# Seven units of yield behind the sample softmax, earlier high casts, and norm vectors on the load queue

## The chip, the cores and the metric

The kernel runs on one core of a Trainium2 chip. A core has TensorE (PE, matmuls and transposes), VectorE (DVE), ScalarE (ACT), GpSimd (POOL) and SyncE (SP); SP, ACT and POOL also issue DMA transfers, each from its own queue in program order. The metric is the device time in microseconds (us) of one execution, as a median of several.

## What is computed

One decoder layer for a prompt of 1024 tokens and a group of 8 x 4 sample tokens with a paged cache of 1024 tokens each. All in f32.

```python
aq, ak, av, bq, bk, bv, iq, ik, iw = split(rms_norm(x, g_mix) @ w_in)
# q, k of A and B: rms_norm per head of 64 (norm vectors q_norm_a, k_norm_a,
# q_norm_b, k_norm_b), then rotary positions; iq, ik: rotary positions
a_out = dsa_attention(aq, iq, iw, ik)   # softmax over the 256 best keys by
        # sum_h iw[h] * relu(iq[h] . ik), a top-k per query row
b_out = diff_attention(bq, bk, bv, lam) # softmax(q1 k1) - lam * softmax(q2 k2)
b_out = rms_norm(b_out, subln) * (1 - lam_init)
h = x + concat(a_out, b_out) @ w_out
y = h + hier_moe(rms_norm(h, g_ffn))    # 4 groups of 8 experts, 2 per token
```

The outputs are y and the new keys and values, of prompt and samples.

## The kernel before

A product in f32 is made of high and low parts: ACT casts a weight chunk to its high part (`wh`, L508), DVE (for one chunk of eight POOL) subtracts to get the low part (`wl`, L530), and PE runs high x high, high x low and low x high (L532, L533, L535 or L538).

**Projections, up to 465 us.** The columns of `w_in` come in sections of 512 columns: BV, the indexer's, BK, AV, BQ, AK, AQ. `section` (L500) casts its 8 chunks, then goes over the 8 prompt tiles of 128 tokens and evacuates each with `evac` (L372): ACT copies the PSUM result, norms and rotary positions follow on DVE and POOL (`m`, L340, and the norm vectors times the rotary table, `gtab`, L176, on POOL), and the last multiply with the reciprocal norm (L387) is POOL's in the two Q sections and DVE's in the K sections. The weights of a section are loaded on SP (`load_w`, called by `preload`) while the one before runs its next to last tile. `gains` loads a section's norm vector, three transfers on ACT's queue, held by `issue_after` until a copy. Beside the sections runs the selection of A's keys (scores, a bisection on POOL, DVE and ACT, and its end, L676 to L701); `mix` takes turns between such streams: it always advances the one whose sum of yields, divided by its total, is smallest. Behind AQ come the first transfers of attention: `open_pages` gathers pages of the cache on POOL's queue, and the queue of stores held back in `late` is emptied on SP (L1041).

**Attention, 465 to 931 us.** Two streams with a total of 280 each are mixed. `prompt_attention` runs B, then A, 8 query tiles each with 4 units per tile (scores L936 and L937 on PE, maxima on DVE, exp L940 on ACT, transposes L876, values L974 or L978), and writes each tile's result (`mo`, L1008, to `s_mix`, L1009 on SP). `samples` runs `sample_attention` for B and A: transposes of the queries and new keys (L1080, L1081) and their copies into `QB` (L1086) and `KN` (L1089), then for each of 2 groups the transposes of the pages (L1104), scores with `QB` (L1112) and with `KN` (L1120), the softmax (exp L1151 on ACT), its transposes (L876, `sc`), and values (`own`, L1165, L1169). Behind both it loads `w_out` through two buffers `raw` (L1219, 16 transfers on SP), casts the high parts (L1220, ACT) and subtracts the low parts (L1221, DVE).

**Output projection and router, 931 to 1079 us.** At its start ACT casts the samples' result `mixS` to its high part `msh` (L1282). The samples are projected first (L1325 to L1327).

**Experts, 1079 to 1402 us.** 24 groups; the weights stream in by DMA.

The order of the instructions on each engine is fixed before the program runs; it follows the order in which the streams are advanced.

Of the kernel before, what the change touches and what calls it, by code (L numbers as in the profile page):

```python
# [6 lines left out]
F32 = mybir.dt.float32  # L7
F32R = mybir.dt.float32r
# [4 lines left out]
ALU = mybir.AluOpType  # L13
# [109 lines left out]
def build(tc, a, upto=99, dbg=None):  # L123
# [185 lines left out]
    def gains(name, ap):  # L309

        g2 = tp.tile([P, 2, 64], F32, name="g2")
        with tc.issue_after(last_copy[0]):
            S.dma_start(g2[:, 0, :], bcast_row(ap[0], 64))
            S.dma_start(g2[:, 1, 0:32], bcast_row(ap[0, 32:64], 32))
            S.dma_start(g2[:, 1, 32:64], bcast_row(ap[0, 0:32], 32))
        gb[name] = g2

    def w2(name):
# [53 lines left out]
    def evac(sec, t, ps):  # L372
        r0, n = rows(t)
        att = sec[0]
        if sec[1] in "KQ":
            raw = w2("raw")
            S.copy(raw[:n], ps[:n])
            rr = tp.tile([P, 8], F32, name="rk")
            rms8(raw, n, rr[:n])
            tab = table(t, sec)  # L380
            ko = outs(t)
            rope(raw, n, 8, tab, ko, V)
            if sec[1] == "Q":

                V.tensor_scalar(rr[:n], rr[:n], 0.125 if t == NT else -0.125, None, op0=ALU.mult)
            E = G if sec[1] == "Q" and t < NT else V
            E.tensor_tensor(out=hd(ko[:n]), in0=hd(ko[:n]), in1=rr[:n].unsqueeze(2).to_broadcast([n, 8, 64]), op=ALU.mult)  # L387
            if sec[1] == "K":
                store(kd[att][r0:r0 + n], ko[:n])
            else:  # L390
                for u in range(2 if t < NT else 1):
                    store(qd[att][r0:r0 + n, :, u, :], hd(ko[:n]), 4)
        else:
            vn = outs(t)
            last_copy[0] = S.copy(vn[:n], ps[:n]).ins
            store(vd[att][r0:r0 + n], vn[:n])
# [70 lines left out]
    def score_tile(t):  # L467
# [29 lines left out]
        V.tensor_tensor(out=score[t][:, t * P:], in0=score[t][:, t * P:], in1=C("caus"), op=ALU.add)  # L497
        yield W * 0.0011

    def section(sec, ws, after=(), prep=False):  # L500

        WLG = (7,)
        evacuate = evac_iq if sec == "I" else lambda t, ps: evac(sec, t, ps)
        first = 2 if sec == "I" else 0
        wh, wl = [], []
        for kc in range(KC):
            wh.append(wp.tile([P, 512], F32R, name="wh", bufs=8))
            S.copy(wh[kc], ws[kc])  # L508
        for t in range(first, NT):
            if prep:  # L510
                if t + 2 < NT:
# [24 lines left out]
            if t == first:  # L536
                for kc in range(KC):
                    T_.matmul(ps, lhsT=xh[t][:, kc, :], rhs=wl[kc], start=False, stop=kc == KC - 1)  # L538
                s4 = w2("s4")
                S.copy(s4, smp)  # L540
                ps2 = acc()
                T_.matmul(ps2[:NS], lhsT=C("sum4"), rhs=s4, start=True, stop=True)
                evacuate(NT, ps2)
            evacuate(t, ps)
            if prep:
                evac_ik(t)
# [190 lines left out]


    SECS = ('BK', 'AV', 'BQ', 'AK', 'AQ')
    nxt = {}  # L740

    def preload(sec):
        def f():
            nxt[sec] = load_w(OFF[sec])
        return (f,)

# [40 lines left out]

    def sections():
        for i, sec in enumerate(SECS):
            if sec[1] != "V":  # L790
                gains(sec, a[f"{sec[1].lower()}_norm_{sec[0].lower()}"])
            yield from section(sec, nxt[sec], preload(SECS[i + 1]) if i + 1 < len(SECS) else (open_pages,))

    p2s = ExitStack()
# [88 lines left out]
    def prompt_attention(atts):  # L883
# [151 lines left out]
        V.tensor_tensor(out=le[:, 0:1], in0=le[:, 1:2], in1=le[:, 0:1], op=ALU.subtract)  # L1035
        V.tensor_scalar(neglam, le[:, 0:1], -0.2, None, op0=ALU.add)
        yield from advance(1, 1)

        while late:
            with tc.issue_after(holds[1]):  # L1040
                Y.dma_start(*late.pop(0))  # L1041
        behind = behind2 = None
        for i in range(len(tiles)):
            cur = nxt
            for u in range(4):
                ex = yield from scores(cur, u)
# [12 lines left out]
            if cur.t == NT - 1:  # L1059
                if behind2:  # L1060
                    yield from values(*behind2)
                behind2 = yield from turned(*behind)
                yield from values(*behind2)
                behind = behind2 = None
            yield from advance(i + 1, 99, True)
            before = cur
        yield from finish(before)

    def sample_attention(att):
# [5 lines left out]
            Y.dma_start(hd(qn[:NS]), qd[att][r0:r0 + NS, :, 0, :])  # L1075
            Y.dma_start(kn[:NS], kd[att][r0:r0 + NS])
        Y.dma_start(vn, vd[att][r0:r0 + NS])
        pt = tr()
        for c in range(4):
            T_.transpose(pt[:, c * NS:(c + 1) * NS], qn[:NS, c * P:(c + 1) * P], ident[:NS, :NS])  # L1080
            T_.transpose(pt[:, (4 + c) * NS:(5 + c) * NS], kn[:NS, c * P:(c + 1) * P], ident[:NS, :NS])  # L1081
        QB = sp_.tile([P, 4, 8, 8, 4], F32, name="QB", bufs=1)
        G.memset(QB, 0.0)
        for c in range(4):
            for s in range(2):
                V.tensor_copy(QB[64 * s:64 * s + 64, c, :, 2 * c + s, :],  # L1086
                              pt[64 * s:64 * s + 64, c * NS:(c + 1) * NS].rearrange("p (b q) -> p b q", q=4))
        KN = sp_.tile([P, 4, NS], F32, name="KN", bufs=1)
        V.tensor_copy(KN.rearrange("p c n -> p (c n)"), pt[:, 4 * NS:8 * NS])  # L1089
        kc_, vc_ = pages(att, "k"), pages(att, "v")  # L1090
        om = []
        for g in range(2):
            sc = sp_.tile([P, NTOK], F32, name="sc", bufs=1)

            for ch in range(4):
                raws = [early.pop(0) if early else page(kc_, ch, 4 * g + bb) for bb in range(4)]
                kts = []
                for r in range(2):
                    for bb in range(4):
# [5 lines left out]
                        evac_any(kt, pt.rearrange("p (c n) -> p c n", n=P))  # L1105
                        kts.append(kt)
                        yield 0.4
                sp = tr()
                for r in range(2):
                    for c in range(4):  # L1110
# [41 lines left out]
            S.activation(ex[:, 1024:], new, AF.Exp, bias=m2[:, 2:3], scale=1.0, accum_out=l2[:, 1:2])  # L1152
            V.tensor_tensor(out=l2[:, 2:3], in0=l2[:, 0:1], in1=l2[:, 1:2], op=ALU.add)
            V.reciprocal(l2[:, 3:4], l2[:, 2:3])
            pT = yield from transposed(ex, 8, "pT")
            ptn = tr()
            T_.transpose(ptn[:NS, :P], ex[:, 1024:], ident)
# [42 lines left out]
            V.tensor_copy(mixS[:, 4:8, :].rearrange("p c n -> p (c n)"), pt[:, :4 * NS])  # L1200

    p3w = ExitStack()
    woh, wol = [], []

    def samples():
        for att in "BA":
# [9 lines left out]
        for k in range(KC):  # L1216
            for q in range(2):
# [3 lines left out]
                V.tensor_tensor(out=wol[q][k], in0=w, in1=woh[q][k].bitcast(F32), op=ALU.subtract)  # L1221
                yield 1.5
        raw.close()

    mix((prompt_attention("BA"), 280), (samples(), 280))
    if "mix" in dbg:
# [50 lines left out]
    p3 = ExitStack()  # L1277
    fp = p3.enter_context(tc.tile_pool(name="fp", bufs=2, reuse_waits="tile"))
    sm = p3.enter_context(tc.tile_pool(name="sm", bufs=2, reuse_waits="tile"))
    msh = sm.tile([P, 8, NS], F32R, name="msh", bufs=1)  # L1280
    msl = sm.tile([P, 8, NS], F32R, name="msl", bufs=1)
    S.copy(msh, mixS)  # L1282
    V.tensor_tensor(out=msl, in0=mixS, in1=msh.bitcast(F32), op=ALU.subtract)
    ovi = cq.tile([P, NT + 1, 2], I32, name="ovi")
    ovv = cq.tile([P, NT + 1, 2, 3], I32, name="ovv")
    T2 = own()
# [18 lines left out]
    def project(t):  # L1305
# [7 lines left out]
            S.copy(mh, mx)  # L1313
            gtt(ml, mx, mh.bitcast(F32), ALU.subtract)
        else:
            mh, ml = msh, msl
        h = fp.tile([P, D], F32, name="xt")
        Y.dma_start(h[:n], xsrc(t))
        s1 = sm.tile([P, 4], F32, name="s1")
# [307 lines left out]
```

## Time and profile before

| | us |
|---|---|
| median of 3 timed runs | 1391.77 |
| lowest and highest of them | 1391.52, 1400.56 |
| the profiled execution | 1403.95 |
| its span, first to last instruction | 1402.1 |
| PE in use in the span | 1265.0 |
| DVE, ACT, POOL in use | 792.0, 561.5, 447.8 |

The profile's page has the busy time of each engine, and a chain of work that ended last; the share of PE in it is 44%. The trace behind the page can be asked for the same by stretches (windows), for an engine's waits and what ended them, and for an engine's instructions one by one (timeline). All times below are of the one profiled execution. A granted clock of 1.00 is PE's full level.

### The profile page before, as it was taken

To read this page: it belongs to the slowest core of one execution; us is meant where nothing else is said; L and a number is where in the kernel's file an instruction comes from. 1 tells how busy PE (TensorE), PEld (TensorE's weight loads), DVE (VectorE), ACT (ScalarE), POOL (GpSimd) and SP (SyncE) were. 2 spreads that over 40 slices of the span, in tenths; PEclk is the share of its full clock that TensorE was granted. 3 is DMA by queue.
4 is the path that set the end of the run, shared out by engine and by line. 5 is a ranking of instruction groups with operands and counts; after the bars stand their busy time and mean duration, and the time that the engine had idled before them with its cause. 6 is when DMAs were issued, how large, how long until landed. Compare 5 with 4: busy or idle time off the path is not lost.

```text
span 1402.1 us, 24778 instructions
## 1 busy us (share of the span) xinstructions
PE 1265.0 (90%) x9359; PEld 855.0 (61%) x9359; DVE 792.0 (56%) x2218; ACT 561.5 (40%) x1239; POOL 447.8 (32%) x505
## 2 busy tenths in 40 slices
PE   7999999997799689898889989999996999999994
PEld 4877675875467576776675776768884333333341
DVE  5544996969987677766655556946754111111110
ACT  5533666895432365544345555732220111111110
POOL 1012233254336534435236544321212112222101
PEclk9999999998899899999899999999997999999997
DMA  6223004133325765666467654347657999999992
GB/s 234 77 88 109 25 24 121 48 109 82 90 97 147 227 244 213 234 210 230 152 227 252 222 161 148 103 135 306 247 172 256 341 370 377 377 381 386 378 340 47
DMA packets 114149, 279.92 MB, mean 200 GB/s; under 512 B 50664, under 2 KB 50920, under 8 KB 101736
## 3 DMA queue, kind: packets, MB, share of 16 engines
q1 hardware_dynamic: 81248, 180.84, 35.4%
q0 software_dynamic: 26272, 95.43, 21.8%
q10 hardware_dynamic: 6504, 2.01, 0.6%
q8 instruction: 75, 1.23, 0.3%
q14 instruction: 50, 0.41, 0.1%
HBM read 234.33 MB, written 43.92 MB: 198 GB/s over the span
## 4 chain that ended last, share of the span: by engine, by line
PE 44%; DMA 9%; DVE 6%; issue 5%; POOL 3%; ACT 2%; SPq 0%; another core or an unknown queue 0%; POOLq 0%; ACTq 0%; DVEq 0%
PE acc L1513 9%; PE S L1533 4%; DMA wg<-in_w_exp_up_dram 4%; PE tr L1104 4%; PE tr L876 3%; PE acc L1325 3%; PE acc L1326 2%; PE acc L1327 2%; PE tr L1112 2%; PE own L1165 2%; PE acc L978 2%; DMA wg<-in_w_exp_gate_dram 2%; PE acc L974 2%; PE tr L936 2%; PE tr L937 2%
## 5 line engine op out<-in xcount | busy, mean ns | idle before, releaser
L532 PE MATMUL acc<-wh,xh 128*128 128x512 f32 x432 | 174.9, 405 | 15.3 <-ACT wh L508 15.3
L1513 PE MATMUL acc<-wg,xT 128*32 128x512 f32 x1536 | 174.7, 598 | 2.8 <-DMA wg<-in_w_exp_up_dram 2.4
L533 PE MATMUL acc<-wh,xl 128*128 128x512 f32 x432 | 172.1, 398 | 0.0
L940 ACT ACTIVATE mk<-mk,mx 128x256 f32<-128x256 f32 (+7 forms) x128 | 99.0, 775 | 83.4 <-DVE mx L938 74.0
L535 PE MATMUL acc<-wl,xh 128*128 128x512 f32 x320 | 126.6, 396 | 0.0
L1513 PEld LDWEIGHTS acc<-wg,xT 128*32 128x32 f32 x1536 | 54.6, 110 | 104.2 <-issue 95.5
L532 PEld LDWEIGHTS acc<-wh,xh 128*128 128x128 f32 x432 | 82.4, 191 | 48.0 <-ACT wh L508 25.8
L1528 DVE COPY aTe<-tr 128x256 f32<-128x256 f32 x24 | 10.2, 425 | 162.6 <-PE tr L1526 162.6
L533 PEld LDWEIGHTS acc<-wh,xl 128*128 128x128 f32 x432 | 82.5, 191 | 17.4 <-issue 1.2
L1533 PE MATMUL S<-wd,aTe 128*32 128x512 f32 x768 | 87.5, 594 | 4.3 <-DVE aTe L1528 3.3
L1508 DVE TENSOR_TENSOR xT<-tr,gc 128x512 f32<-128x512 f32 x48 | 32.9, 688 | 91.5 <-PE tr L1507 91.5
L1104 PE MATMUL tr<-cst,pg 128*128 128x128 f32 x512 | 78.8, 286 | 0.5 <-DVE ql L407 0.4
L936 PE MATMUL tr<-KS,qh 128*128 128x512 f32 (+3 forms) x192 | 75.1, 396 | 1.6 <-DVE aT L864 0.8
L1519 ACT ACTIVATE sg<-acc,its 128x256 f32<-128x256 f32 x24 | 11.4, 474 | 156.0 <-PE acc L1513 156.0
L1537 POOL DMA_INDIRECT out_o_y_dram<-yo,its x24 | 38.0, 1582 | 110.2 <-ACT yo L1536 66.1
L958 POOL TENSOR_SCALAR mk<-mk,rl 128x128 f32<-128x128 f32 (+7 forms) x64 | 49.3, 781 | 70.9 <-DVE rl L950 65.8
L1498 POOL DMA_INDIRECT xg<-s_hn,its x24 | 23.4, 977 | 142.4 <-PE tr L1507 128.9
L876 PE MATMUL tr<-cst,mk 128*128 128x128 f32 x432 | 65.1, 281 | 4.0 <-POOL mk L958 2.4
L535 PEld LDWEIGHTS acc<-wl,xh 128*128 128x128 f32 x320 | 60.9, 190 | 11.8
L937 PE MATMUL tr<-KS,ql 128*128 128x512 f32 (+3 forms) x192 | 66.2, 359 | 0.0
L1536 ACT ACTIVATE yo<-S,its 128x1024 f32<-128x1024 f32 x24 | 26.8, 1115 | 98.5 <-PE S L1533 98.5
L1104 PEld LDWEIGHTS tr<-cst,pg 128*128 128x128 f32 x512 | 61.6, 147 | 6.5 <-issue 2.0
(416 smaller groups left out, 2924.2 us busy)
## 6 DMA issues: line engine op xcount, KB each, us to landing
wg<-in_w_exp_gate_dram SPq DMA_DIRECT2D x32, 1024.0 KB
wg<-in_w_exp_up_dram SPq DMA_DIRECT2D x32, 1024.0 KB
wd<-in_w_exp_down_dram SPq DMA_DIRECT2D x32, 1024.0 KB
wr<-in_w_in_dram SPq DMA_DIRECT2D x56, 256.0 KB
xt<-in_x_prompt_dram SPq DMA_DIRECT2D x16, 512.0 KB
s_mix<-mo SPq DMA_DIRECT2D x16, 256.0 KB
qn<-s_qa SPq DMA_DIRECT2D x8, 512.0 KB
raw<-in_w_out_dram SPq DMA_DIRECT2D x16, 256.0 KB
```

The costliest lines, as they stand in the source:

```text
L532: T_.matmul(ps, lhsT=xh[t][:, kc, :], rhs=wh[kc], start=kc == 0 and t < NT - 1, stop=False)
L533: T_.matmul(ps, lhsT=xl[t][:, kc, :], rhs=wh[kc], start=False, stop=t == NT - 1 and kc == KC - 1)
L535: T_.matmul(ps, lhsT=xh[t][:, kc, :], rhs=wl[kc], start=False, stop=kc == KC - 1)
L876: T_.transpose(pt[:, (j - b) * P:(j - b + 1) * P], src[:, j * P:(j + 1) * P], ident)
L936: T_.matmul(sp[:, :c1 - c0], lhsT=T.qh[:, h * P:(h + 1) * P], rhs=KS[:, h, c0:c1], start=True, stop=False)
L937: T_.matmul(sp[:, :c1 - c0], lhsT=T.ql[:, h * P:(h + 1) * P], rhs=KS[:, h, c0:c1], start=False, stop=True)
L940: S.activation(mk[:, :W], mk[:, :W], AF.Exp, bias=mx[:, h:h + 1], scale=-1.0, accum_out=T.ll[:, h:h + 1])
L958: G.tensor_scalar(ex[s][:, :W], ex[s][:, :W], T.rl[:, 2 * u + s:2 * u + s + 1], 1.0, op0=ALU.mult, op1=ALU.mult)
L1104: T_.transpose(pt[:, c * P:(c + 1) * P], raws[bb][:, o_:o_ + P], ident)
L1325: T_.matmul(ps[:n], lhsT=mh[:, k, :], rhs=woh[q][k], start=k == 0, stop=False)
L1513: T_.matmul(gu[c:c + m, :].rearrange("p (u f) -> p u f", u=2), lhsT=xT[:, k, c:c + m], rhs=wg[:, :, k, :], start=k == 0, stop=k == KC - 1)
L1533: T_.matmul(py[c:c + m, q * 512:(q + 1) * 512], lhsT=aT[:, k, c:c + m], rhs=wd[:, k, q * 512:(q + 1) * 512], start=k == 0, stop=k == 1)
```

## The change

- `gains` issues on SP, without `issue_after`, and is called in `preload`, that is, one section earlier, ahead of the section's weights.
- In `evac` the last multiply of AQ's prompt tiles is DVE's; BQ's stays on POOL.
- `high` casts chunks of a section on demand: the first four of the next section are cast ahead of the evacuation of the last tile.
- The stores left in `late` are issued at the second prompt tile, in a plain loop.
- The queries' transposes and the `QB` and `KN` copies of the samples move behind the first eight page transposes.
- `yield 7` stands between the samples' exp and its transposes.
- The cast of `mixS` (now `ms`) moves from the start of the projection to the end of `samples`, behind the loads of `w_out`.

```diff
     def gains(name, ap):
         g2 = tp.tile([P, 2, 64], F32, name="g2")
-        with tc.issue_after(last_copy[0]):
-            S.dma_start(g2[:, 0, :], bcast_row(ap[0], 64))
...
+        Y.dma_start(g2[:, 0, :], bcast_row(ap[0], 64))
...
-            E = G if sec[1] == "Q" and t < NT else V
+            E = G if sec == "BQ" and t < NT else V
...
+    def high(ws, b, e):
+        got = whs.setdefault(id(ws), [])
+        for kc in range(b, e):
+            if len(got) == kc:
+                got.append(wp.tile([P, 512], F32R, name="wh", bufs=8))
+                S.copy(got[kc], ws[kc])
+        return got
...
-        wh, wl = [], []
-        for kc in range(KC):
-            wh.append(wp.tile([P, 512], F32R, name="wh", bufs=8))
-            S.copy(wh[kc], ws[kc])
+        wh, wl = high(ws, 0, KC), []
...
+            if t == NT - 1 and after and nxt_of(sec):
+                high(nxt[nxt_of(sec)], 0, 4)
             evacuate(t, ps)
...
     def preload(sec):
         def f():
+            if sec in SECS and sec[1] != "V":
+                gains(sec, a[f"{sec[1].lower()}_norm_{sec[0].lower()}"])
             nxt[sec] = load_w(OFF[sec])
...
-        while late:
-            with tc.issue_after(holds[1]):
-                Y.dma_start(*late.pop(0))
...
         for i in range(len(tiles)):
             cur = nxt
+            while i == 1 and late:
+                Y.dma_start(*late.pop(0))
...
+        def queries():
+            G.memset(QB, 0.0)
+            pt = tr()
...
+                if g == 0 and ch == 0:
+                    queries()
                 sp = tr()
...
             V.reciprocal(l2[:, 3:4], l2[:, 2:3])
+            yield 7
             pT = yield from transposed(ex, 8, "pT")
...
         raw.close()
+        mp = p3w.enter_context(tc.tile_pool(name="ms", bufs=1, side="right", reuse_waits="tile"))
+        msh, msl = [mp.tile([P, 8, NS], F32R, name=f"ms{u}") for u in range(2)]
+        S.copy(msh, mixS)
+        V.tensor_tensor(out=msl, in0=mixS, in1=msh.bitcast(F32), op=ALU.subtract)
+        ms.extend((msh, msl))
...
-    msh = sm.tile([P, 8, NS], F32R, name="msh", bufs=1)
...
-    S.copy(msh, mixS)
```

Three places in the order of the engines follow. Line numbers of the changed kernel are up to 23 higher (L876 of before is L890 there, L936 is L950).

PE, samples of A, first group, of before: from the last sample scores (`KN`, `QB`) to the first transposes of the exponentials (`sc`).

```order
L1120 MATMUL tr<-KN,QB 32x32 x16
L920 MATMUL tr<-idr,kst 128x128 x8
L1130 LDWEIGHTS repb
L1130 MATMUL tr<-selS,repb 128x512
L1130 LDWEIGHTS repb
L1130 MATMUL tr<-selS,repb 128x512
L1134 LDWEIGHTS repb
L1134 MATMUL tr<-selS,repb 128x32
L876 MATMUL tr<-cst,sc 128x128 x4
```

The same place of the change, the last eleven of the 33 rows that stand between: a prompt unit's scores (`KS`), values (`aT`, `VV`) and mask transposes (`mk`).

```order
L950 MATMUL tr<-KS,qh 128x384
L951 MATMUL tr<-KS,ql 128x384
L950 MATMUL tr<-KS,qh 128x384
L951 MATMUL tr<-KS,ql 128x384
L992 MATMUL acc<-aT,VV 64x128 x6
L890 MATMUL tr<-cst,mk 128x128 x6
L950 MATMUL tr<-KS,qh 128x512
L951 MATMUL tr<-KS,ql 128x512
L950 MATMUL tr<-KS,qh 128x512
L951 MATMUL tr<-KS,ql 128x512
L890 MATMUL tr<-cst,sc 128x128 x4
```

Where the sample scores were followed by seven rows of little work, several prompt units now stand ahead of `sc`.

POOL at the end of section AQ, of before: `m` and the multiplies (L387) of the last tiles, page gathers (`pg`), and the first key cast of attention (`kst`).

```order
L387 TENSOR_TENSOR outs<-outs,rk 128x512
L340 TENSOR_TENSOR m_5056<-raw,gtab 128x512
L387 TENSOR_TENSOR outl<-outl,rk 128x512
L340 TENSOR_TENSOR m_5106<-raw,gtab 128x512
L554 DMA pg<-in_cache_b_k_dram,row_78 128x1024 x2
L387 TENSOR_TENSOR outl<-outl,rk 128x512
L1083 MEMSET QB 128x1024
L176 TENSOR_TENSOR kst<-first,kst 128x8x64
```

The same of the change.

```order
L176 TENSOR_TENSOR gtab<-rot,g_4558 128x128
L339 TENSOR_TENSOR m_5056<-raw,gtab 128x512
L339 TENSOR_TENSOR m_5106<-raw,gtab 128x512
L563 DMA pg<-in_cache_b_k_dram,row_78 128x1024
L1096 MEMSET QB 128x1024
L176 TENSOR_TENSOR kst<-first,kst 128x8x64
```

The multiplies have left POOL, and one gather stands there instead of two.

ACT at the end of the prompt's attention, of before: from the last casts of `w_out` (`woh`) to the last exps (`mk`) of the prompt's last tile, 7; the `mo` copy is that of tile 6.

```order
L1220 CAST woh_9946<-raw 128x512
L940 ACTIVATE mk,ll<-mk,mx 128x1024
L1220 CAST woh_9962<-raw 128x512
L940 ACTIVATE mk,ll<-mk,mx 128x1024
L1008 COPY mo<-acc 128x512
L862 COPY aT<-tr 128x512
L940 ACTIVATE mk,ll<-mk,mx 128x1024 x2
L862 COPY aT<-tr 128x512 x3
L940 ACTIVATE mk,ll<-mk,mx 128x1024 x4
```

The same end of the change, from the exps of tile 7 to the cast of `mixS`; the `mo` copy is that of tile 7.

```order
L954 ACTIVATE mk,ll<-mk,mx 128x1024
L876 COPY aT<-tr 128x512
L1241 CAST woh_10348<-raw 128x512
L876 COPY aT<-tr 128x512 x2
L1314 DMA gc<-in_g_ffn_dram 128x8
L1241 CAST woh_10333<-raw 128x512
L876 COPY aT<-tr 128x512
L1241 CAST woh_10349<-raw 128x512
L1241 CAST woh_10334<-raw 128x512
L1022 COPY mo<-acc 128x512
L1241 CAST woh_10350<-raw 128x512
L1241 CAST woh_10335<-raw 128x512
```

One more `woh` cast and the cast of `mixS` follow. Before, all 16 casts stand ahead of tile 6's `mo`; in the change 2 stand ahead of it, 11 between it and tile 7's, and 3 behind. On SP the 16 loads are split by the stores `s_mix` in the same way: 4, then 11, then the last behind tile 7's store.

## Rows read from the trace of the kernel before

**Rows 1.** Windows: stretch, its length, busy us of each engine, granted clock, DMA share, GB/s.

```profile
467.00:469.00 2.00, 1.04 (x10) 0.80 (x8) 0.42 (x1) 0.00 (x0) 2.00 (x2) 1.00 0.00 0
473.00:486.00 13.00, 5.43 (x24) 5.09 (x25) 8.35 (x24) 3.47 (x8) 5.40 (x6) 0.65 0.95 326
865.00:909.00 44.00, 40.89 (x364) 33.15 (x366) 40.50 (x97) 30.79 (x60) 16.74 (x15) 1.00 0.34 103
909.00:931.00 22.00, 20.86 (x218) 17.33 (x214) 13.24 (x45) 11.67 (x22) 7.15 (x7) 1.00 0.04 14
1079.00:1402.00 323.00, 296.36 (x2544) 111.67 (x2544) 53.82 (x96) 39.43 (x49) 58.24 (x47) 0.96 0.92 333
```

**Rows 2.** Waits of PE from 320 to 430: releaser, total us, times, longest.

```profile
PE acc L532 <- ACT wh L508: 15.3, 3, 9.5
```

**Rows 3.** Timeline of ACT: start, us, instruction, idle before it and its releaser.

```profile
345.86 0.61 ACT L697 ACTIVATE sjunk<-score,selst 128x384 bf16<-128x384 f32 x1 [4.68 <-DVE selst L693]
...
346.89 0.82 ACT L697 ACTIVATE sjunk<-score,selst 128x640 bf16<-128x640 f32 x1
```

**Rows 4.** Timeline of POOL in section BQ.

```profile
296.26 0.88 POOL L176 TENSOR_TENSOR gtab<-rot,g 128x128 f32<-128x128 f32 x2 [1.90 <-DMA g<-in_q_norm_b_dram]
```

**Rows 5.** End of AQ: timelines of POOL, ACT, DVE, PE; multiplies of line L387.

```profile
467.91 1.26 POOL L340 TENSOR_TENSOR m<-raw,gtab 128x512 f32<-128x512 f32 x1
...
472.03 1.05 POOL L387 TENSOR_TENSOR outl<-outl,rk 128x512 f32<-128x512 f32 x1
...
473.93 1.27 POOL L176 TENSOR_TENSOR kst<-first,kst 128x512 fp32r<-128x512 f32 x1
...
465.42 0.57 ACT L377 COPY raw<-acc 128x512 f32<-128x512 f32 x1
...
469.21 0.69 DVE L342 TENSOR_TENSOR raw<-raw,gtab 128x512 f32<-128x512 f32 x1 [1.79 <-POOL m L340]
...
475.25 1.11 PE L920 MATMUL tr<-idr,kst 128*128 128x128 f32 x4 [7.21 <-ACT le L1034]
...
L387 DVE TENSOR_TENSOR outs<-outs,rk x8: 677/688/693, 145.8 to 413.6; 128x512 f32<-128x512 f32 x8
```

**Rows 6.** Line L1086: ns least, median, most; first and last start.

```profile
L1086 DVE COPY QB<-tr x16: 172/194/1264, 474.0 to 679.2; 64x32 f32<-64x32 f32 x16
```

**Rows 7.** Waits of PE from 486 to 940; timeline of PE at the longest.

```profile
PE tr L876 <- ACT sc L1151: 11.6, 4, 5.0
...
734.38 1.11 PE L876 MATMUL tr<-cst,sc 128*128 128x128 f32 x4 [5.00 <-ACT sc L1151]
```

**Rows 8.** Windows behind three of these waits, columns as in rows 1.

```profile
634.30:640.00 5.70, 5.62 (x36) 3.57 (x37) 2.31 (x7) 0.91 (x4) 0.86 (x1) 0.74 0.12 27
734.30:741.00 6.70, 6.62 (x36) 4.09 (x37) 3.16 (x11) 1.79 (x8) 0.74 (x2) 0.60 0.06 21
832.10:837.00 4.90, 4.81 (x29) 3.79 (x33) 2.88 (x11) 1.85 (x6) 0.00 (x0) 0.68 0.00 0
```

**Rows 9.** Timelines of PE, ACT and DVE from the last `own` to the projection.

```profile
863.90 1.06 PE L1169 MATMUL own<-vns,pn 32*32 32x512 f32 x8
...
931.83 0.42 PE L1325 MATMUL acc<-woh,msh 128*32 128x512 f32 x1 [0.98 <-ACT msh L1282]
...
869.60 1.14 ACT L1220 CAST woh<-raw 128x512 fp32r<-128x512 f32 x2
...
875.89 0.62 ACT L1220 CAST woh<-raw 128x512 fp32r<-128x512 f32 x1 [0.55 <-DMA raw<-in_w_out_dram]
...
904.72 0.62 ACT L1220 CAST woh<-raw 128x512 fp32r<-128x512 f32 x1
909.53 0.59 ACT L1008 COPY mo<-acc 128x512 f32<-128x512 f32 x1 [2.84 <-PE acc L978]
...
930.89 0.59 ACT L1008 COPY mo<-acc 128x512 f32<-128x512 f32 x1 [3.19 <-PE acc L978]
...
871.94 0.68 DVE L1221 TENSOR_TENSOR wol<-raw,woh 128x512 fp32r<-128x512 f32 x1
```

More of the change, by code (lines that the diff above doesn't have):

```diff
@@ L311, in gains @@
         g2 = tp.tile([P, 2, 64], F32, name="g2")
-        with tc.issue_after(last_copy[0]):
-            S.dma_start(g2[:, 0, :], bcast_row(ap[0], 64))
-            S.dma_start(g2[:, 1, 0:32], bcast_row(ap[0, 32:64], 32))
-            S.dma_start(g2[:, 1, 32:64], bcast_row(ap[0, 0:32], 32))
+        Y.dma_start(g2[:, 0, :], bcast_row(ap[0], 64))
+        Y.dma_start(g2[:, 1, 0:32], bcast_row(ap[0, 32:64], 32))
+        Y.dma_start(g2[:, 1, 32:64], bcast_row(ap[0, 0:32], 32))
         gb[name] = g2
@@ L498, in score_tile @@
         yield W * 0.0011
+    whs = {}
+    def high(ws, b, e):
[5 more added lines that the diff above has]
+        return got
     def section(sec, ws, after=(), prep=False):
@@ L739, in build, with nxt_of @@
     SECS = ('BK', 'AV', 'BQ', 'AK', 'AQ')
+    ALL = ("BV", "I") + SECS
     nxt = {}
+    def nxt_of(sec):
+        i = ALL.index(sec) + 1
+        return None if i == len(ALL) else "IQ" if ALL[i] == "I" else ALL[i]
     def preload(sec):
         def f():
+            if sec in SECS and sec[1] != "V":
+                gains(sec, a[f"{sec[1].lower()}_norm_{sec[0].lower()}"])
             nxt[sec] = load_w(OFF[sec])
@@ L789, in sections @@
         for i, sec in enumerate(SECS):
-            if sec[1] != "V":
-                gains(sec, a[f"{sec[1].lower()}_norm_{sec[0].lower()}"])
             yield from section(sec, nxt[sec], preload(SECS[i + 1]) if i + 1 < len(SECS) else (open_pages,))
@@ L1077, in sample_attention @@
         Y.dma_start(vn, vd[att][r0:r0 + NS])
[L1078 to L1081, printed above, removed]
         QB = sp_.tile([P, 4, 8, 8, 4], F32, name="QB", bufs=1)
[L1083 to L1087, printed above, removed]
-        KN = sp_.tile([P, 4, NS], F32, name="KN", bufs=1)
-        V.tensor_copy(KN.rearrange("p c n -> p (c n)"), pt[:, 4 * NS:8 * NS])
+        KN = sp_.tile([P, 4, NS], F32, name="KN", bufs=1)
+        def queries():
+            G.memset(QB, 0.0)
+            pt = tr()
+            for c in range(4):
+                T_.transpose(pt[:, c * NS:(c + 1) * NS], qn[:NS, c * P:(c + 1) * P], ident[:NS, :NS])
+                T_.transpose(pt[:, (4 + c) * NS:(5 + c) * NS], kn[:NS, c * P:(c + 1) * P], ident[:NS, :NS])
+            for c in range(4):
+                for s in range(2):
+                    V.tensor_copy(QB[64 * s:64 * s + 64, c, :, 2 * c + s, :],
+                                  pt[64 * s:64 * s + 64, c * NS:(c + 1) * NS].rearrange("p (b q) -> p b q", q=4))
+            V.tensor_copy(KN.rearrange("p c n -> p (c n)"), pt[:, 4 * NS:8 * NS])
         kc_, vc_ = pages(att, "k"), pages(att, "v")
@@ L1202, in build @@
     p3w = ExitStack()
-    woh, wol = [], []
+    woh, wol, ms = [], [], []
     def samples():
@@ L1279, in build @@
     sm = p3.enter_context(tc.tile_pool(name="sm", bufs=2, reuse_waits="tile"))
-    msh = sm.tile([P, 8, NS], F32R, name="msh", bufs=1)
-    msl = sm.tile([P, 8, NS], F32R, name="msl", bufs=1)
-    S.copy(msh, mixS)
-    V.tensor_tensor(out=msl, in0=mixS, in1=msh.bitcast(F32), op=ALU.subtract)
     ovi = cq.tile([P, NT + 1, 2], I32, name="ovi")
@@ L1315, in project @@
         else:
-            mh, ml = msh, msl
+            mh, ml = ms
         h = fp.tile([P, D], F32, name="xt")
```

## The prediction

> **What bounds the kernel now.** I read the windows of engine busy time first, then the waits of TensorE (PE), then the engines' timelines at those waits, last the queue of each engine in program order. From 1079 us on the expert stage keeps the DMA share at 0.92 [rows 1]; the change touches nothing there but its start. So the sum is made of PE's idle stretches before, and of the clock after them: a microsecond by which the attention ends earlier or later moves the end by as much. The profiled execution took 1403.95 us, 12.2 above the median of the timed runs, 1391.77. The differences below hold for either, and I forecast the median.
>
> **Norm vectors on the load queue, casts ahead.** Three waits of PE for ACT's high casts L508, at the start of section AK, cost 15.3 us [rows 2]. ACT's first cast there stood behind a selection instruction L697 that had waited for DVE's `selst` until 345.86, 4.68 us [rows 3]; the norm loads of the next section stand ahead of that in ACT's queue, but ACT was waiting anyway. The reordered casts find no better place: in the changed order a second selection instruction, 0.82 us, precedes the first cast [rows 3], and the others follow as before. Gain 0, loss at most 0.8. What the loads do change is section BQ: POOL waited 1.90 us for the norm vector at 296.26, with steps of the selection's bisection behind it on POOL [rows 4]. Loaded a section earlier, that wait goes, and if the selection's end and with it AK's stall come earlier by as much, 1.9 us are won. I take -2, bounds +0.8 (something else holds the selection) and -4 (twice the wait, if an evacuation step moves forward as well). [...]
>
> **AQ's last multiply from POOL to DVE.** At the end of AQ, POOL runs a product m (1.26 us) and a multiply (1.05) for each tile; DVE waits 1.79 us for m [rows 5]. The last multiply ended at 473.08, `kst` behind it started at 473.93, and PE waited 7.21 us for `kst` until 475.25 [rows 5] (the page names ACT as releaser, but `kst` ends last). Without the multiply, m of the last tile can start when ACT's copy ends, 465.42 + 0.57 = 465.99, instead of 467.91: 1.9 us, and another 1.05 goes ahead of `kst`. On DVE the multiply takes 0.69 [rows 5], inside the 1.79 that it waited. So `kst`, and the stores with the loads behind them on SP, come 3.0 us earlier. From 473 to 486 the DMA share is 0.95, but from 467 to 469 it is 0.00 [rows 1], so the whole batch can shift. I take -3, bounds -1 (a transfer takes back most of it) and -5 (the four QB copies that leave this place add to it). [...]
>
> **Queries later.** The eight QB copies on DVE take 0.19 us each as a median [rows 6], 1.6 us together. In attention B they lay in a stretch where PE was waiting; now they stand directly ahead of the first matmul that reads them. At B and at A I take half of it each and the transposes, +1, so +2; bounds 0 and +4.
>
> **Seven units of prompt work behind each sample softmax.** PE waited four times for the sample exp L1151, 11.6 us together, the longest 5.00 until 734.38 [rows 7]. Before, only the mask broadcasts and one key transpose lie between the last sample scores and the `sc` transposes. After, there are 16 score matmuls, 22 mask transposes, 16 value products and 16 other transposes at the longest wait: 70 matmuls, which at the 40.89 us for 364 of the stretch from 865 on [rows 1] make 7.9 us. All four waits can close. [...] The term is -17.4; bounds -7 (half of the waits come back as waits of the work put in, with half of the clock) and -17.4 itself.
>
> **What the same units delay: w_out.** Both streams have 280 as their total, so each yield sets the sample stream back by 7, 28 in all. Before, the last sample value product `own` ended at 864.96; the 16 loads of w_out follow it, and the last cast started at 904.72, long before PE's first projection matmul at 931.83 [rows 9]. After, that `own` stands in tile 7. PE work left behind it: the rest of tile 6 (28 values, 14 mask transposes, 8 scores and their 28 values, 78 instructions at 0.112 us by the ratio above, 8.7 us) and that of tile 7 between the two copies of `mo`, 909.53 to 930.89, 21.4 us: 30.1 in all; with the 0.98 us wait for the cast of the sample's result [rows 9], projection would start at own + 31.1. The loads run in two buffers, their last cast began 39.8 us behind own; after its 0.62 comes the cast of the sample's result, 0.4, which now stands behind cast 16 on ACT. Projection starts at own + 40.8: +9.7. Should loads land faster now that the DMA share is as low as the 0.04 from 909 on, against 0.34 [rows 1], a round of two buffers is some 3.3 us of load (from 872.62, the buffer free, to 875.89, the cast that waited for it), 0.62 of cast and 0.68 of subtraction [rows 9], 4.6 us; the measured one is (35.1 - 0.6) / 7 = 4.9 (869.60 to 904.72, seven rounds and one cast). Seven rounds save 2.1: +7.6. I take +8.5, and as PE idles before the projection +1.5 for the clock, the least of [rows 8]: +10.
>
> **Sum.** -2 - 3 + 2 - 17.4 + 10 = -10.4: 1393.5 for the profiled execution, 1381 for the median.
>
> **Rivals.** (a) **The tail is covered:** the loads land fast and tile 7, with ACT and DVE fuller, ends later by itself, so that only the last cast and the sample's result show, +2 instead of +10: 1373. For it: DMA is nearly idle there. Against: a cast before waited 0.55 us for its load in a queue that was a third full. (b) **The stall moves:** the prompt work put in is itself a chain of transposes, ACT exps and DVE maxima; if PE waits for it in the same place, -7 is left of -17.4 and the time is 1391.8, no change. For it: the prompt's tiles have the same dependences; against: from 865 to 931, with little sample work, PE was in use for 61.8 of 66 us [rows 1]. (c) **Slower: casts and exps hold each other up in tile 7.** In ACT's order casts 3 to 13 stand between tile 7's exps, each waits for its load, and PE, DVE and the next buffer wait behind. If a round takes 2.5 us more (two exps of tile 7 stand between the casts of a round), seven rounds cost 17.5 more and the sum is +7: 1399. It decides from 1.5 us more per round, where the sum passes 0.
>
> **How the numbers follow.** The forecast has 0.50, own range 1376 to 1388; (a) 0.25, (b) 0.13, (c) 0.12. About 1% is what a measurement of this kernel can tell from no change, here 13.9 us. Faster by more begins below 1377.9: all of (a) and a fifth of the forecast, 0.35. Slower begins above 1405.7: (c) with the unknown costs at their upper bounds, 0.09. Within 1% lies the rest, 0.56. The range of 1371 to 1398 leaves out the far ends of (a) and (c).
>
> **What would show it.** Right: no wait of PE for the sample exp above 1 us, and a clock near 1 behind it; the idle stretch before `kst` shorter by some 3 us; w_out's last cast behind the prompt's last value product, and a wait of the first projection matmul for ACT of 5 to 10 us; AK's waits smaller by 2. Wrong: casts done before tile 7 ends (a); new waits of PE for `mk` or `aT` of more than 5 us (b); waits of tile 7 for exps behind casts (c). A change in the expert stage's own length, which I hold constant, would break the sum.

## The result and the profile after

The changed kernel takes 1402.47 us (median of 14 executions, 1400.41 to 1404.4), the kernel before 1394.65 beside it (also 14): ratio 1.0052, 95% interval 1.0040 to 1.0064. That is 7.3 us slower, where 10.4 us faster was forecast; 1381 lies far below, and the range ended at 1398. On the 1391.77 of three executions from which the prediction counted, the ratio makes 1399.0.

| | before | after |
|---|---|---|
| median, us | 1394.65 | 1402.47 |
| profiled execution, us | 1403.95 | 1404.4 |
| its span, us | 1402.1 | 1402.6 |
| PE in use, us | 1265.0 | 1269.7 |

The two profiled executions differ by less than the medians do: that of before was 9 us above its median, that of after 2 us. So whole spans of these two traces can't be compared; waits can. The runs below were made on several chips, on which the kernel before takes 1373 to 1401 us; each of their ratios is to the kernel before on the same chip, and 0.001 is 1.4 us.

Waits of PE after, from 465 to 960 us (waiting matmul, releaser, total, times, longest):

```profile
PE acc L1348 <- ACT ms L1248: 7.3, 1, 7.3
PE tr L1131 <- issue: 7.1, 19, 1.0
PE tr L1220 <- DVE bo L1217: 6.0, 1, 6.0
PE tr L1015 <- DVE bo L1011: 6.0, 3, 3.0
PE tr L934 <- POOL kst L176: 3.7, 1, 3.7
PE acc L992 <- ACT aT L876: 3.2, 3, 1.5
PE tr L890 <- DVE mk L969: 3.1, 2, 2.0
```

The wait of [rows 7] for the sample exp (11.6 us) has gone altogether. In its place stand waits for `bo`, the results of B that DVE normalizes (before: 3.2 and 1.6 us), and 7.3 us at the first projection matmul. Waits of the masks `mk`, which the prediction had named as a sign, grew less: 6.0 us, before 3.7. Around the first projection matmul, the timelines of ACT and PE:

```profile
907.41 0.62 ACT L1241 CAST woh<-raw 128x512 fp32r<-128x512 f32 x1 [4.23 <-DMA raw<-in_w_out_dram]
907.94 1.15 ACT L954 ACTIVATE mk<-mk,mx 128x1024 f32<-128x1024 f32 x1
...
921.60 0.58 ACT L1022 COPY mo<-acc 128x512 f32<-128x512 f32 x1 [2.51 <-PE acc L992]
...
927.05 0.62 ACT L1241 CAST woh<-raw 128x512 fp32r<-128x512 f32 x1 [2.33 <-DMA raw<-in_w_out_dram]
928.43 0.41 ACT L1248 CAST ms<-mixS 128x256 fp32r<-128x256 f32 x1 [0.76 <-DVE wol L1242]
...
881.70 1.06 PE L1190 MATMUL own<-vns,pn 32*32 32x512 f32 x8
...
928.89 0.63 PE L1348 MATMUL acc<-woh,ms 128*32 128x512 f32 x1 [7.33 <-ACT ms L1248]
```

In [rows 9] the last cast of w_out began at 904.72, 27 us ahead of the projection. Here it begins at 927.05, 5.5 us behind tile 7's last result (`mo`, 921.60); one exp of tile 7 stood behind a cast that waited 4.23 us for its load. Two windows there (columns as in rows 1):

```profile
900.00:929.00 29.00, 17.52 (x158) 14.30 (x154) 16.65 (x42) 12.75 (x23) 6.27 (x5) 0.80 0.42 127
929.00:943.00 14.00, 14.00 (x53) 6.20 (x54) 1.34 (x3) 2.04 (x4) 2.53 (x1) 0.81 0.78 245
```

PE is in use for 17.5 of 29 us and then runs the samples' projection at a granted clock of 0.81; before, all of this ran at 1.00 (900 to 931.8, and the samples' projection from 931.83 to 943).

At the start of attention the multiply's move did what was forecast (POOL and PE, to be compared with [rows 5]):

```profile
465.99 1.28 POOL L339 TENSOR_TENSOR m<-raw,gtab 128x512 f32<-128x512 f32 x1 [4.20 <-issue]
...
469.78 1.27 POOL L176 TENSOR_TENSOR kst<-first,kst 128x512 fp32r<-128x512 f32 x1
...
471.10 1.11 PE L934 MATMUL tr<-idr,kst 128*128 128x128 f32 x4 [3.73 <-POOL kst L176]
477.98 1.09 PE L403 MATMUL tr<-cst,qn 128*128 128x128 f32 x4 [2.22 <-DMA qn<-s_qb]
```

The last m starts at 465.99, where ACT's copy had ended before (in this execution the copy ends at 465.87), and PE has the keys at 471.10 instead of 475.25. In two tiles ahead of the last, a multiply that now runs on DVE and POOL's m overlap, and the one that starts second takes longer than alone (POOL and DVE):

```profile
446.24 1.74 POOL L339 TENSOR_TENSOR m<-raw,gtab 128x512 f32<-128x512 f32 x1
455.06 1.29 POOL L339 TENSOR_TENSOR m<-raw,gtab 128x512 f32<-128x512 f32 x1 [0.65 <-ACT raw L376]
...
446.00 0.83 DVE L386 TENSOR_TENSOR outl<-outl,rk 128x512 f32<-128x512 f32 x1
455.08 1.82 DVE L386 TENSOR_TENSOR outs<-outs,rk 128x512 f32<-128x512 f32 x1
```

The first m starts while DVE multiplies and takes 1.74 us instead of 1.29; the second m starts first, and DVE's multiply takes 1.82 instead of 0.69. The last m, ahead of `kst`, met no multiply and took 1.28.

And a wait is there that the prediction did not name, in section BK: norm loads on SP, a gather of indexer keys on POOL, and PE waiting for it.

```profile
208.83 0.34 SPq L312 DMA_DIRECT2D g<-in_k_norm_a_dram  x1
209.22 0.42 SPq L313 DMA_DIRECT2D g<-in_k_norm_a_dram  x1
209.69 0.42 SPq L314 DMA_DIRECT2D g<-in_k_norm_a_dram  x1
...
208.95 1.26 POOL L563 DMA_INDIRECT ikp<-in_cache_idx_k_dram,row  x1 [0.15 <-issue]
...
215.07 1.11 PE L585 MATMUL tr<-cst,ikp 128*128 128x128 f32 x4 [2.04 <-DMA ikp<-in_cache_idx_k_dram,row]
```

### The profile page after: what moved, and what is told of

Its sections match the earlier page's. It is cut to its first block, busy times and chain, and to the rows that moved or that the text cites. A ratio compares the mean times of both kernels' runs of the same rounds, so it can differ in the third digit from the quotient of the medians.

```text
span 1402.6 us, 24784 instructions
## 1 busy us (share of the span) xinstructions
PE 1269.7 (91%) x9359; PEld 859.2 (61%) x9359; DVE 794.4 (57%) x2226; ACT 560.9 (40%) x1239; POOL 442.4 (32%) x497
## 5 line engine op out<-in xcount | busy, mean ns | idle before, releaser
L538 PE MATMUL acc<-wh,xh 128*128 128x512 f32 x432 | 175.0, 405 | 15.7 <-ACT wh L506 15.7
L950 PE MATMUL tr<-KS,qh 128*128 128x512 f32 (+3 forms) x192 | 73.5, 387 | 1.5 <-ACT aT L876 1.1
L890 PE MATMUL tr<-cst,mk 128*128 128x128 f32 x432 | 67.3, 286 | 7.3 <-DVE mk L969 3.1
L878 DVE COPY aT<-tr 128x512 f32<-128x512 f32 (+3 forms) x86 | 46.1, 555 | 47.7 <-PE tr L890 34.4
L339 POOL TENSOR_TENSOR m<-raw,gtab 128x512 f32<-128x512 f32 x32 | 48.0, 1502 | 61.8 <-ACT raw L376 45.1
```

Source lines behind the costliest of these rows:

```text
L339: last_rot[0] = (V if n == NS else G).tensor_tensor(out=m2[:n, :w].rearrange('p (h u d) -> p h u d', u=2, d=32), in0=sv[:, :, ::-1, :], in ...
L538: T_.matmul(ps, lhsT=xh[t][:, kc, :], rhs=wh[kc], start=kc == 0 and t < NT - 1, stop=False)
L878: V.tensor_copy(out, in_)
L890: T_.transpose(pt[:, (j - b) * P:(j - b + 1) * P], src[:, j * P:(j + 1) * P], ident)
L950: T_.matmul(sp[:, :c1 - c0], lhsT=T.qh[:, h * P:(h + 1) * P], rhs=KS[:, h, c0:c1], start=True, stop=False)
```

## The experiments

**The kernel before once more.**

> The kernel before once more, for a second trace. Its first profiled execution took 1403.95 us and its timed median is 1394.65, 9.3 less; the changed kernel's took 1404.4 against 1402.47. Theory A: the first trace of before held a stretch of about 9 us that most of its executions do not have, and a second trace of a time near 1394 shows which (a stage that is 5 to 9 us shorter). Theory B: the profile itself costs the kernel before 9 us and the changed one 2; then this trace is again near 1404 and stage by stage like the first to within 1 us.

It took 1372.57 us, on a chip where its median was 1373.97: its profiled execution is no slower than the rest, so theory B is out. Theory A is not shown, since the chip is another one and the whole difference is larger than 9 us. Its attention, from the last projection matmul to the first of the output projection, lasts 437.7 us, against 466.9 in the first trace; the sections ahead and the experts behind are alike to within 2 us. In the first trace PE also waits 10.8 us "for nothing that the profile shows" at the sample scores, here less than 0.5. So attention is the part whose length differs between these two traces.

**Without the yields; with the yields alone; with the yields and a faster sample stream.**

```diff
-            yield 7                       # first kernel, from the change
```
```diff
             V.reciprocal(l2[:, 3:4], l2[:, 2:3])
+            yield 7                       # second, to the kernel before
```
```diff
-    mix((prompt_attention("BA"), 280), (samples(), 280))
+    mix((prompt_attention("BA"), 280), (samples(), 323))   # third
```

> The changed kernel without the line yield 7. Theory A (the yields put the loads of w_out into the prompt's last tile, and what they cost there is more than the sample exp's waits gave back): faster than the changed kernel by some 3 to 8 us, ratio to before 0.998 to 1.002; the four waits for the sample exp are back with about 11 us, the wait of the first projection matmul for the cast of the samples' result is below 1 us. Theory B (the yields gain and another part of the change loses): slower than the changed kernel, ratio to before above 1.008.

> The kernel before with the line yield 7 alone. Theory A: it carries the loss, ratio to before 1.003 to 1.007, with a wait of 5 to 10 us at the first projection matmul and tile 7 of the prompt held up by casts of w_out. Theory B: it is faster than before, ratio 0.990 to 0.997, and the other parts of the change lose 10 us and more.

> The changed kernel with 323 instead of 280 as the total of the sample stream, so that it runs relatively faster by its longer sum of yields and ends where it ended before the change; the yields stay. Theory A (the tail is the loss): no wait above 1 us at the first projection matmul, the sample exp's waits below 3 us, 8 to 12 us faster than the changed kernel: ratio to before 0.996 to 1.000. Theory B (the loss lies ahead of the tail): within 2 us of the changed kernel, ratio 1.004 to 1.007.

Ratios to before: 0.9998 (0.9989 to 1.0007), 1.0047 (1.0034 to 1.0060), 0.9992 (0.9979 to 1.0005). By the ratios theory A in all three: the yields carry the loss, 6.5 us by themselves, and with the stream's end back in its old place it is gone. But the third says more than was asked. It has the yields without the tail, and is only 0.8 us faster than the kernel without yields, with an interval of some 2.2 us either way. Waits of PE in attention, first without yields, then with the faster stream:

```profile
PE tr L890 <- ACT sc L1170: 11.9, 4, 4.5
PE tr L934 <- POOL kst L176: 3.7, 1, 3.7
PE tr L1219 <- DVE bo L1216: 3.2, 1, 3.2
PE acc L992 <- ACT aT L876: 2.6, 4, 1.2
PE tr L403 <- DMA qn<-s_qb: 2.5, 1, 2.5
PE tr L890 <- POOL mk L972: 2.4, 5, 0.7
PE acc L988 <- DVE bo L1011: 1.7, 2, 1.0
PE tr L890 <- DVE mk L969: 1.5, 2, 1.1
```

```profile
PE tr L890 <- POOL mk L972: 5.5, 3, 4.2
PE tr L934 <- POOL kst L176: 3.7, 1, 3.7
PE tr L890 <- DVE mk L969: 3.6, 4, 1.4
PE tr L1220 <- DVE bo L1217: 3.2, 1, 3.2
PE acc L988 <- DVE bo L1011: 3.1, 4, 1.3
```

11.9 us of waits for `sc` have left; waits for the prompt's own `mk` and `bo` have grown by about 7, from 8.8 to 15.4 in the rows shown.

**The changed kernel beside the price of the waits, the price of the loads, and the multiply put back.**

```diff
-            pT = yield from transposed(ex, 8, "pT")
+            pT = yield from transposed(None, 8, "pT")   # None: reads cst[:, :P]
```
```diff
             for q in range(2):
+                if q:
+                    woh[1][k], wol[1][k] = woh[0][k], wol[0][k]
+                    yield 1.5
+                    continue
```
```diff
-            E = G if sec == "BQ" and t < NT else V
+            E = G if sec[1] == "Q" and t < NT else V   # without the yields
```

> The changed kernel once more, on the chip of the runs beside it. Theory A (yields cost by their tail, the rest of the change is worth nothing): ratio to before 1.003 to 1.006, as the yields alone had 1.0047 and the change without them 0.9998. Theory B (its first comparison mixed chips): below 1.002.

> The changed kernel without the yields, and with the sample softmax's transposes reading a constant tile that is ready, so that PE never waits for the sample exp (the exp itself still runs; the samples' attention weights are left out of the output). It prices the four waits in place. Theory A (the waits of 11.9 us and the low clock behind them are worth what they last): 10 to 17 us faster than the change without yields, ratio to before 0.987 to 0.993. Theory B (another chain paces attention, so that a wait closed here comes back at the next transposes, copies or loads): at most 4 us faster, ratio 0.997 to 1.000, and PE's waits for mk, aT, bo or for the clock grow by 8 us and more.

> The changed kernel with 8 of the 16 loads of w_out left out, and their casts and subtractions (the second half of w_out is taken equal to the first). The yields stay, the chain of loads behind the last own is half as long. Theory A (the tail is paced by the loads): no wait above 1 us for the cast of the samples' result, no wait of tile 7 for casts, 6 to 10 us faster than the changed kernel, ratio to before 0.997 to 1.000. Theory B (the yields lose ahead of the tail): within 2 us of the changed kernel.

> The changed kernel without the yields and with AQ's last multiply back on POOL. Theory A (the move is worth what PE's first waits of attention lost, 3.5 us for kst and 1.8 for the queries): 3 to 5 us slower than the change without yields (0.9998), ratio 1.002 to 1.004. Theory B (page gathers pace that stretch, and the start of attention gives it back): same within 1.5 us, ratio 0.999 to 1.001, with kst later by 3 us and the end of attention where it was.

The changed kernel: 1.0025 (1.0007 to 1.0042), a little under its first ratio, with the interval just reaching theory A. With the waits closed by ready data: 0.9926 (0.9905 to 0.9946), 9 to 10 us below the kernel without yields (0.9998 on one chip, 0.9991 on another): theory A, just short of its 10 to 17 us. With half of the loads: 0.9925 (0.9904 to 0.9945), 14 us below the changed kernel, more than theory A's 6 to 10. With the multiply back on POOL: 1.0024 (1.0009 to 1.0039), 3.6 to 4.6 us above the kernel without yields: theory A. The kernel without yields was not timed on the chip of these four, so these two differences go across chips. As the third leaves out casts and subtractions too, the next four separate these.

**Yields and loads, two by two, on one chip.** The kernels are those above, and the fourth is that with half of the loads, without the yields.

> First of four kernels that stand beside each other on one chip: the changed kernel, with and without the yields, each with 16 and with 8 loads of w_out. This is the changed kernel as it is: ratio to before 1.002 to 1.006 by both theories.

> Second of the four: without the yields, 16 loads. Both theories: 0.998 to 1.001.

> Third of the four: with the yields, 8 loads (second half of w_out taken equal to the first, so the output differs). Both theories: 0.991 to 0.996, as it had 0.9925 before.

> Fourth of the four: without the yields, 8 loads. Theory A (the yields by themselves gain about what the waits for the sample exp last, and the late loads of w_out take it back): close to the kernel without yields and 16 loads, since its loads lie beside other work, ratio 0.997 to 1.000, so that at 8 loads the yields gain 5 to 10 us and at 16 loads they lose 4 to 7; the difference of the two, 10 to 15 us, is the tail. Theory B (the yields gain nothing, the loads left out free ACT, DVE and the DMA queues in both kernels alike): as fast as the third, ratio 0.991 to 0.995.

| ratio to before | 16 loads | 8 loads |
|---|---|---|
| with the yields | 1.0044 (1.0026 to 1.0062) | 0.9934 (0.9917 to 0.9951) |
| without | 0.9991 (0.9977 to 1.0004) | 0.9955 (0.9939 to 0.9971) |

Between A and B. The loads left out save 5 us also in the kernel without yields, where PE had no wait above 1 us for them. The yields cost 7.4 us with 16 loads and gain 2.9 with 8; the difference, 0.0074 or 10.3 us, is the tail. Its interval, from the four, is some 4.5 us either way; that of the gain of 2.9 is 3.3, so it isn't clear of zero. With 8 loads and yields PE has no wait for the cast of the samples' result, but two casts in tile 7 still wait for their loads, 2.10 and 1.51 us, so a little of the tail may be left there.

**Which yields, the norm loads, and the parts that gained together.**

```diff
+            if att == "A":                # second kernel "A", third "B"
                 yield 7
```
```diff
-            E = G if sec[1] == "Q" and t < NT else V   # fourth, to the kernel before
+            E = G if sec == "BQ" and t < NT else V
...
+            if att == "A":
+                yield 4
             pT = yield from transposed(ex, 8, "pT")
```

The first has the lines of `gains` and its call as they stood before, and no yields.

> The changed kernel without the yields, and with the norm vectors loaded from ACT's queue at the old place again. Theory A (the small descriptors of k_norm_a, issued on SP at 209 us, hold up a gather of indexer keys issued by POOL at 209.2, for which PE then waits): PE's waits for ikp fall from 4.9 us back below 1 us, POOL waits about 2 us for q_norm_b again, and the kernel is 2 to 4 us faster than with the loads on SP (0.998 to 1.000): ratio to before 0.996 to 0.998. Theory B (the selection paces that part up to AK's end, the delay is made up there): same as without yields, 0.998 to 1.000.

> The changed kernel with the yields in attention A alone, 14 units in all, so that the last loads of w_out still lie beside the prompt's last tile. Theory A (the two waits in A, 8.2 us and the low clock behind them, are filled by the larger tiles of that part; those in B are not): ratio to before 0.993 to 0.997. Theory B (every yield only moves its wait): 0.998 to 1.001.

> The changed kernel with the yields in attention B alone, 14 units. Theory A (in B the prompt's tiles are small, their own chain of norms over bo is left bare when the samples pause): the two waits of 4.3 us for the sample exp go, waits for bo and mk of 5 us and more come, ratio to before 0.998 to 1.002. Theory B (as good as in A): 0.993 to 0.997.

> The kernel before with two things of the change: AQ's last multiply on DVE, and a yield of 4 units, in attention A alone. By the parts as measured so far (the multiply 3 to 5 us, the waits of A some 5, no tail): ratio to before 0.992 to 0.996. If the yields in A are worth nothing: 0.996 to 0.999.

Norm loads back on ACT: 0.9996 (0.9982 to 1.0010), theory B. PE's waits for `ikp` have gone from its list, POOL's for q_norm_b has come back (1.83 us), and the time is that of 0.9998, within 2.3 us. Its trace does differ up to AQ's end: that POOL wait, and a window behind the place where PE waited for `ikp`, first of the changed kernel, then of this one:

```profile
293.29 0.88 POOL L176 TENSOR_TENSOR gtab<-rot,g 128x128 f32<-128x128 f32 x2 [1.83 <-DMA g<-in_q_norm_b_dram]
...
216.00:220.00 4.00, 4.00 (x11) 3.13 (x11) 1.50 (x2) 2.04 (x4) 0.00 (x0) 0.50 0.48 117
...
216.00:220.00 4.00, 4.00 (x25) 2.93 (x25) 3.41 (x9) 3.05 (x6) 1.08 (x1) 1.00 0.96 300
```

With the loads on SP the granted clock is 0.50 in that window, behind the wait; here it is 1.00. The last projection matmul ends at 461.7 us, in the two traces beside it with the loads on SP (yields in A, yields in B) at 464.7 and 464.2. One trace each, and the medians do not show it: a price of 2 to 3 us is neither shown nor excluded. Yields in A alone: 0.9992 (0.9979 to 1.0005), theory B. Yields in B alone: 1.0037 (1.0023 to 1.0052), slower even than theory A had it. Its waits of PE in attention:

```profile
PE tr L890 <- ACT sc L1170: 6.8, 2, 4.1
PE tr L1015 <- DVE bo L1011: 6.7, 4, 3.0
PE tr L1221 <- DVE bo L1218: 5.4, 1, 5.4
PE acc L992 <- ACT aT L876: 3.9, 3, 2.4
```

The `sc` row is that of A alone (2 waits); 4.2 us in B have gone. All waits for `bo` together were 5.6 us without yields and are 12.6 here: 7 us have come. The kernel of before with the multiply on DVE and 4 units in A: 0.9920 (0.9904 to 0.9937), 1362.24 us against 1374.32. In the part that holds attention A, 640 to 850 us, the largest waits of the kernel without yields, then of this one:

```profile
PE tr L890 <- ACT sc L1170: 7.7, 2, 4.5
PE tr L1219 <- DVE bo L1216: 3.2, 1, 3.2
PE tr L890 <- POOL mk L972: 1.7, 3, 0.7
```

```profile
PE tr L1201 <- DVE bo L1198: 3.2, 1, 3.2
PE tr L876 <- POOL mk L958: 3.1, 4, 1.3
PE tr L936 <- DVE KS L864: 1.2, 2, 1.0
```

Here 7.5 us go (0.2 is left) and 2.6 come back, 1.4 for `mk` and 1.2 for `KS`; the last cast of w_out starts at 873.26 and is done 16 us ahead of the prompt's last `mo`.

**The queries, and a version of the change with its gaining parts.**

```diff
-                if g == 0 and ch == 0:
-                    queries()
...
+        queries()
         kc_, vc_ = pages(att, "k"), pages(att, "v")
```

The first kernel has this and no yields; the second has it, the norm loads at their old place, and 4 units in A.

> The changed kernel without the yields, and with the samples' query transposes and the QB and KN copies at their old place, at the start of each sample attention. Theory A (they cost 3 us at their new place, where the first scores wait for them): PE's waits for QB gone, ratio to before 0.996 to 0.998. Theory B (what the multiply gained is lost elsewhere, in the stores or in the norm loads): 0.999 to 1.001.

> The changed kernel with the norm loads and the query copies at their old places and, instead of the seven units, a yield of 4 in attention A alone; the high casts ahead, the multiply on DVE and the early cast of the samples' result stay. Theory A (only the misplaced parts cost): ratio to before 0.989 to 0.994, like the kernel of before with multiply and yield (0.992) or better by the 2 us by which the casts ahead end AQ earlier. Theory B (the casts ahead or the early cast cost too): 0.995 to 0.998.

Queries at their old place: 0.9969 (0.9956 to 0.9982), theory A; against 0.9998 that is 4.0 us, 2.2 either way and across two chips. The second: 0.9931 (0.9910 to 0.9951), theory A, not to be told from 0.9920. So casts ahead, the stores issued at the second tile and the early cast of the samples' result together neither gain nor cost anything that can be measured. Both kernels with 4 units in A are faster than before by 9 to 11 us, and than the change by 13 to 18, by which of its three ratios is taken.

## Why the prediction was wrong

**Norm vectors, casts ahead (-2): 0, within its bounds.** PE's waits for the high casts are 15.7 us, against 15.3 in [rows 2], so the casts found no better place, as said. POOL's wait of [rows 4] went, but it did not carry through to AK. What came instead I had not priced: three transfers of k_norm_a on SP, issued within a microsecond of a gather on POOL's queue, and PE waited 2.04 us for that gather. The trace shows this order in time, not what held the gather up. With the loads back, PE's wait and the clock of 0.50 behind it were gone and POOL's wait was there again (1.83 us), but the total stayed; what each is worth in the end is not shown.

**AQ's multiply (-3): right.** Back on POOL it costs 3.6 to 4.6 us. Last m 465.99 as worked out, `kst` 4.15 us earlier (3.0 said; one gather fewer stands ahead of it), both waits smaller by 3.5 and 2.7. In two earlier tiles m and the multiply overlap, and the one that started second took longer (0.45 us more for m, 1.13 more for the multiply), but not in the last tile, whose m, 1.28 us, is the one on the way to `kst`; the term is what the move is worth with these overlaps.

**Queries (+2): 4.0, at the upper bound.** What I counted were the copies; PE's waits for `QB` in the changed kernel are only some 2 us in all, so half of the price is not seen as a wait on them. That it is the place, ahead of work that both streams need, is not shown.

**The seven units (-17.4): this step failed.** That all four waits would close was right: none is left. But I booked their whole length and the clock behind three of them (0.60 to 0.74 in [rows 8]) as gain, and in the term itself booked nothing for what would stand in their place. Measured, the yields without their tail gain 0.8 us (faster sample stream) to 2.9 us (8 loads), with intervals that reach zero. (Half of the waits and half of the clock, as the lower bound was put, would be -8.7 and not -7; either is far from what was measured.) That the waits themselves were worth their time is shown by the kernel that closes them with ready data and moves nothing: 9 to 10 us faster. So the price of the waits was sound, that of the clock not shown, and the exchange failed: the gain came back elsewhere.
- *The wait moves.* While the samples pause, the prompt runs alone, and its own chains stand bare: the normalization of B (`bo`), the mask chain (`mk`). Some 7 of 11.9 us came back so. By the waits alone 5 us should be left, and 0.8 to 2.9 were measured; what takes the rest is open, within the intervals. In B it is a loss: 4.2 us of waits for 7 of `bo`, and 1.0037. This was rival (b), held at 0.13 because the prompt alone ran well from 865 on [rows 1]; but that stretch holds the last tiles of A, up to tile 7, with the largest units and no `bo`. I took the best stretch of one attention for the other.
- *Where and how long.* In A, 4 units close the waits (7.5 us go, 2.6 come) and gain: 0.9931 against 0.9969 on the same chip, 5.2 us with 3.4 either way; the two differ in the norm loads as well, which measured as nothing. Seven in A gave 0.9992, beside 0.9996 without yields and with the norm loads back: 0.5 us, 2.6 either way. That seven is too much by itself is not shown: no run has 7 units in A with the queries at their old place, the waits that came back are about as many (2.9 us), and the two gains differ by 4.7 us with 4.3 either way.
- *The clock.* Of the 17.4, 11.6 are the waits of [rows 7]; the other 5.8 were my estimate, the shortfall of the granted clock from 1.00 over the three stretches of [rows 8]. The 1.5 for the clock in the tail is the least of the same three and is not shown by itself; measured there is 0.81 over 14 us. No run shows the 5.8 as a gain: the mean granted clock of attention is the same, 0.96, without yields and with yields and no tail (first and second row; columns as in rows 1).

```profile
464.10:899.20 435.10, 396.59 (x4004) 315.86 (x4002) 307.91 (x887) 239.37 (x590) 204.49 (x215) 0.96 0.61 208
463.80:901.20 437.40, 403.46 (x4004) 318.47 (x4002) 306.90 (x888) 239.96 (x590) 202.88 (x215) 0.96 0.61 207
```

PE was in use 6.9 us longer with the yields here, but the other pair of traces on that chip has it the other way, 395.5 us in the kernel before and 390.9 with the yields alone; nothing is read from it.

**The tail (+10): right in size, 10.3 by the two by two, with 4.5 either way.** The faster stream, with yields and no such tail, makes it some 7.6 (0.9992 against 1.0047 with the yields alone, on one chip). Its place is right too: the loads of w_out behind the last `own`, which ended at 882.76. Not its make: projection was to begin at own + 40.8 and began at own + 46.1, and tile 7, which I had end at own + 30.1, ended at 921.6, own + 38.8. There rival (c) shows, casts that wait for loads ahead of tile 7's exps on ACT, but it adds to the loads' pace rather than deciding the case: 41.6 us from the first cast to the last, where 35.1 had been measured. That is 0.9 us more per round, and (c) was to decide from 1.5.

**The sum.** With the measured terms, 0 - 4 + 4 - 3 + 10 is +7, and +7.3 was measured. The sum closes almost by itself, since the last two terms are parts of one measured cost of the yields, 7.4 us. The term that failed is the yields' own, -3 at best where -17.4 was put; even the smaller of its bounds, -7, was too much. Rival (c) had the time, 1399, right, for a reason that was only part of it, so that was luck. Rival (b) had the reason: it has the full tail of +10 in its sum, but left -7 for the yields and so came out at no change; what was missing is that almost all of the gain could come back.

## What to carry to other kernels

A wait's length is what closing it is worth only if nothing is moved to close it. When other work is put into a gap, ask what stood beside that work before and is bare now, in that very stretch, and where the stream that was put back ends: here a pause of 4 units in the attention with the large tiles gained some 5 us, and one of 7 in both lost 7, as the late loads took more than the waits had left.

## What the runs showed of the hardware

Attention was longer on some chips than on others. The kernel before has 437.7 us of it in one trace and 466.9 in another, while the stages ahead and behind are alike to 2 us. Over all kernels, ten traces on the chips where the kernel before takes 1373 to 1374 us have 427 to 443 us, and ten on those where it takes 1395 to 1401 have 448 to 467. In the longer of the first two PE waited 10.8 us, in 20 waits at the sample scores, for nothing that the profile shows; what makes the rest is open.

Where a multiply on DVE and a product on POOL, both f32 of 128x512 and of two tiles, overlapped in the trace of the changed kernel, the one that started second took longer: 1.74 us instead of 1.29 on POOL, and 1.82 instead of 0.69 on DVE, one case each.
